# A decoder block on one core: the first adaLN shift group summed by TensorE as columns, its loads in pieces

## Chip, cores and metric

The kernel runs on 1 core of one Trainium2 chip. The metric is the device time of one execution in microseconds (us). The kernel before was timed three times; the median is 1146.56 us.

## What is computed

One decoder block on 256 tokens of width 2048, in float32. A conditioning vector `c` gives six vectors of 2048 values (two shifts, two scales, two gates) through `w_ada`; then come a normalised, scaled and shifted projection `w_in`, eight heads of causal attention beside a gated short convolution, `w_out`, and a gated feed-forward part with a convolution.

```python
mod = jax.nn.silu(c) @ w_ada[l] + b_ada[l]
sh1, sc1, g1, sh2, sc2, g2 = jnp.split(mod, 6, axis=-1)
h = modulate(rms_norm(x, norm1_g[l]), sh1, sc1)      # h * (1 + sc1) + sh1
proj = h @ w_in[l]                                   # 2048 -> 6144
...                                                  # attention | gated convolution, norms
x = x + g1[:, None, :] * (mixed @ w_out[l])
h2 = modulate(rms_norm(x, norm2_g[l]), sh2, sc2)
u = causal_dwconv(h2 @ w_ffn_up[l], ffn_conv_w[l], ffn_conv_b[l])
u_gate, u_up = jnp.split(u, 2, axis=-1)
x = x + g2[:, None, :] * ((jax.nn.silu(u_gate) * u_up) @ w_ffn_down[l])
```

## The kernel before

**Slots.** All weights stream from HBM through seven buffers of 1 MB ("raw"). A weight tile is a *slot*. ScalarE (ACT) rounds it to a high part `hi` (line 329), VectorE (DVE) forms the remainder `lo` (through the wrapper at line 166, under which most DVE work is recorded), and TensorE (PE) makes three products of each block: hi with the high and the low part of the activations, lo with the high part. The first 48 slots are `w_in`, then come 16 of `w_out`, then the feed-forward part. `CFG['turns']` (line 51) lists which columns of the projection (q, k, v, gates g, convolution inputs c and x) the first 48 slots cover, in which order and for which block rows. Slot 0 has its own loop, `go_first` (line 574, matmuls on line 583); later ones use lines 514 to 517.

**The six vectors.** Each of them is cut into groups (class `Ada`, `CFG['ada']`, line 44). A group's tiles are consumed between slots, in one of two ways: by PE (`pe` true: a block of silu(c), repeated over 32 columns, is stationary, the weights move, four row groups at once; line 396) or by DVE, row block by row block (lines 387, 389). `evac` copies a PE group's sums out (line 417), `cols` transposes them by PE (line 453) and sums the four row groups on DVE, so that the values lie along the partitions; B gets shift + bias, A gets (1 + scale) x gain.

**The order.** Everything runs in the order of the program: each engine has one queue. `CFG` sets when a step is placed: `at(i, f)` puts step f at slot i, `cls` puts it before or after that slot's preparation, `x_first` and `hi_late` say for each slot whether adaLN tiles come before the next weights, and whether `hi` is made late. `consume` (a list near the end) is the order of all loads; `load_next` issues the next one on SyncE's queue when a buffer has been given back.

**The head.** Before slot 0 can start, x is loaded and transposed by PE in eight blocks (`xn_tr`), its norm is worked out, and `xn_norm` multiplies each transposed block by it on DVE. In the two groups of `ada_init` (line 1171), the scale SC1 and the shift SH1 of the first 256 columns are summed by PE from two tiles of 1 MB each. SH1 is the last of them (from line 1525): consume its two tiles, `evac`, `cols`; its values z go into `h = hf + z` on ACT (line 1548), where `hf` was made by DVE as x * A1 + bias. Then slot 0's first matmul can go. Slot 0's tile is loaded in two halves (`pair_load`, line 539), and split into hi and lo in two halves, too.

Of the kernel before, what the change touches and what calls it, by code (L numbers as in the profile page):

```python
# [9 lines left out]
F32 = mybir.dt.float32  # L10
F32R = mybir.dt.float32r
AF = mybir.ActivationFunctionType
ALU = mybir.AluOpType
AX = mybir.AxisListType

P = 128
D = 2048
S = 256
NK = D // P
# [9 lines left out]
SH1, SC1, G1, SH2, SC2, G2 = range(6)  # L29
# [11 lines left out]
       'unit_act': [0, 1, 2, 3, 4, 5, 6, 7],  # L41
       'down_turns': [[0, 1, 2], [3]],
       'join': [[-5, 1], [-2, 6]],
       'ada': [[0, 2, 256, False, 0, 5], [2, 0, 2048, False, 26, 22], [5, 0, 2048, False, 40, 32],
# [3 lines left out]
       'bufs': [38, 6, 7, 3, 3],  # L48
       'parked': ['q'],
       'unpark': 56,  # L50
# [5 lines left out]
       'fill': [[3, 12]],  # L56
# [25 lines left out]
               'qk_norm': 0,  # L82
               'out_norm': 0,
               'cols': -1,
               'conv_q': 0,
               'att_q': -1,
               'up_gate': 2,
               'hold_a': 2,
# [7 lines left out]
               'up_conv': 2,  # L96
               'up_conv_b': 2,
               'att_p': 0,
               'ss_part': 0,
               'up_sum': -1,  # L100
               'sq_out': -1,
               'att_s': -1,
               'tr_out': 0,
               'evac': 1,
               'qk_stat': 2,
               'load_x': 1,
               'att_t': 2,
               'att_o': 2,
               'gate_down': 2,
               'conv_g': 1,  # L110
               'conv_c': -1,
               'evac_in': 0,
               'qk_root': 0,
               'evac_out': -1,
               'bias': -1,
               'add_bias': -1,
               'up_silu': 2,
               'ss_cols': -1,
               'sum_rows': 1,
               'evac_sum': -1,  # L120
               'join_load': 0,
               'join_sum': 2},
       'up0': [[1, 1, 2, 4], [0, 1, 3, 3], [0, 2, 1, 2], [1, 1, 3, 5], [4, 4, 5, 8], [5, 5, 6, 9]],
       'la': 2,
       'near': 3,
# [1 line left out]
       'direct': 4,  # L127
       'spill': [6, 9],
       'back': [-2, 0, -1, 1],
       'x_first': [1, 2, 3, 4, 6, 8, 9, 10, 11, 12, 13, 14, 16, 18, 20, 21, 22, 26, 27, 30, 31, 34, 37, 39, 42, 43, 44, 45,  # L130
                   47, 48, 49, 50, 51, 53, 57, 58, 59, 60, 61, 62, 65, 66, 67, 74, 82, 83],
       'h_act': True,
       'h_lag': 0,
       'hi_late': [1, 2, 3, 5, 6, 11, 12, 14, 15, 17, 19, 20, 21, 22, 25, 26, 28, 30, 31, 32, 39, 42, 44, 45, 47, 49, 51,
                   53, 54, 57, 59, 61, 64, 66, 68, 70, 72, 76, 77, 78, 79, 80, 82, 83],
       'first_hi': True,
       'cut': [4, 4, 4],
       'fold': 3,
       'twos': [],
# [8 lines left out]
def tile_block(  # L148
# [5 lines left out]
    nc = tc.nc  # L154
    mm = nc.tensor.matmul
    act = nc.scalar.activation
# [14 lines left out]
    V, W = Vector(), nc.vector  # L171
# [10 lines left out]
    def bank(name):  # L182
        return ps.tile([P, 512], F32, tag="b", bufs=8, name=name)
# [3 lines left out]
    def t2k(name, dt=F32):  # L187
        return sb.tile([P, 512], dt, tag="t2k", bufs=N_T2K, name=name)

    def t1k(name, dt=F32):  # L190
        return sb.tile([P, 256], dt, tag="t1k", bufs=N_T1K, name=name)

    def small(n, name):
        return sb.tile([P, n], F32, tag="small", bufs=16, name=name, padded_shape=[P, 32])
# [64 lines left out]
    def load_next():  # L259
        if not pending:  # L260
            return
        issue, key = pending.pop(0)
        if isinstance(issue, Ada):

            issue.home()
            return
        t = sb.tile([P, 4, 512], F32, tag="raw", bufs=N_RAW, name="raw")
        issue(t)
        ready.append((key, t))

    def take(key):
        n = [k for k, _ in ready].index(key)
        return ready.pop(n)[1]
# [65 lines left out]
    csil = const.tile([P, NK], F32, name="csil")  # L339
    crep = const.tile([P, NK, 32], F32, name="crep")  # L340
    A1 = const.tile([P, NK], F32, name="A1")
# [4 lines left out]
    class Ada:  # L346


        def __init__(self, part, c0, n, pe):
            self.part, self.c0, self.n, self.pe = part, c0, n, pe  # L350
            self.rows = 2048 // n
            self.tiles = NK // self.rows
            self.nch = n // P
            self.acc = None
            self.two = []
            self.used = 0

        def want(self, r):
            a = self.part * D + self.c0 * P
            k0 = r * self.rows  # L360

            def issue(t):
                nc.sync.dma_start(self.view(t), w_ada[0, k0 * P:(k0 + self.rows) * P, a:a + self.n]
                                  .rearrange("(k p) f -> p k f", p=P))
            return issue

        def home(self):
            what = f"ada{self.part}_{self.c0}"
# [112 lines left out]
    def at(i, f, *a):  # L481
        tasks.setdefault(i, []).append((CFG["cls"].get(f.__name__, 0), f, a))

    done = set()
# [3 lines left out]
    hT = {}  # L488
# [5 lines left out]
    COL = {"q0": 0, "q1": 1, "k0": 2, "k1": 3, "v0": 4, "v1": 5, "g0": 6, "g1": 7, "c0": 8, "c1": 9,  # L494
           "x0": 10, "x1": 11}

    def halves(v):
        return v[:, :256], v[:, 256:]
# [21 lines left out]
    for w in CFG["parked"]:  # L520
        q = sb.tile([P, 4, 512], F32, tag="raw", bufs=N_RAW, name="pa_" + w)
# [15 lines left out]
    slots_begun = []  # L537

    def pair_load(k, f):
        def issue(t):  # L540

            n = 1 if not slots_begun else 2
            slots_begun.append(f)
            for j in range(0, 2, n):
                nc.sync.dma_start(t.rearrange("p (k h) f -> p k (h f)", k=2)[:, j:j + n],
                                  w_in[0, (k + j) * P:(k + j + n) * P, COL[f] * 512:COL[f] * 512 + 1024]
                                  .rearrange("(k p) f -> p k f", p=P))
        return issue


    turns, upto = [], {}
# [124 lines left out]
    for n, (f, part, k) in enumerate(seq):  # L676
# [6 lines left out]
        i = len(slots)  # L683
# [411 lines left out]
    for n, (what, *a) in enumerate(CFG["plan"]):  # L1095
        if what == "x":
# [10 lines left out]
            rest = todo  # L1107
# [12 lines left out]
    parts = []  # L1120
    for fs in CFG["down_turns"]:
        k = ka
# [46 lines left out]
        ready_at.update({(g.part, g.c0 + k): s + 2 for k in range(g.nch)})  # L1169

    ada_init = [Ada(SC1, 0, 256, True), Ada(SH1, 0, 256, True)]

    def h_chunks(ks):
        assert all((part, k) in done for k in ks for part in (SC1, SH1))
# [12 lines left out]
    for part, c0 in CFG["fill"]:  # L1187
        g = Ada(part, c0, 512, True)
        fill += [(g, r) for r in range(g.tiles)]
    n0, n1, n2 = CFG["fill_at"]  # L1190
    extra.setdefault(N_OUT - 1, []).extend(fill[:n0])
    fill_a, fill_b = fill[n0:n0 + n1], fill[n0 + n1:n0 + n1 + n2]
    for i, (g, r) in enumerate(fill):
        if i >= n0 + n1 + n2:
            extra.setdefault(N_OUT + (i - n0 - n1 - n2) // 2, []).append((g, r))
        if r == g.tiles - 1:
            a = N_OUT + 1 + max(0, (i - n0 - n1 - n2) // 2)
# [163 lines left out]
    for half in range(2):  # L1361
        for w in "qk":
            at(in_last[f"{w}{half}"], qk_stat, f"{w}{half}")
        i = max(in_last[f"{w}{half}"] for w in "qk")
        at(i + CFG["qk"][half][0], qk_root, half)
        at(i + CFG["qk"][half][1], qk_norm, half)
        n = i + CFG["qk"][half][1]
        for j in range(4):
            h = 4 * half + j
# [82 lines left out]
    for i in range(len(slots)):  # L1452
# [3 lines left out]
        w = [("w", n) for n in ahead(i)]  # L1456
# [29 lines left out]
    xnT, xnP = {}, {}  # L1486
# [13 lines left out]
    g1n, bcol = vbc[:, 0:16], vbc[:, 16:112]  # L1500
# [12 lines left out]
    def xn_norm(*js):  # L1513
        for j in js:
            xnT[j] = t2k(f"xnT{j}")
            V.tensor_tensor(out=xnT[j].rearrange("p (k t) -> p k t", k=2), in0=xnP.pop(j).rearrange("p (k t) -> p k t", k=2),
                            in1=rT.unsqueeze(1).to_broadcast([P, 2, 256]), op=ALU.mult)

    xn_norm(0, 1, 2, 3)
    ada_init[0].consume(1)  # L1520
    ada_init[0].evac()
    ada_init[0].cols()
    xn_norm(4)
    xn_tr(5)
    ada_init[1].consume(0)
    xn_tr(6, 7)
    xn_norm(5, 6, 7)
    ada_init[1].consume(1)
    ada_init[1].evac()

    w = take(("w", 0))
    hi, lo = (sb.tile([P, 4, 512], F32R, tag=g, bufs=N_HL, name=g) for g in ("hi", "lo"))
    parts = [(slice(2 * k, 2 * k + 2), t1k("hf"), t2k(f"h{k}", F32R)) for k in range(2)]
    b1 = SH1 * NK
    for k, (s, h, hk) in enumerate(parts):
        hT[k] = halves(hk)
        V.tensor_scalar(h, xnT[0][:, k * 256:(k + 1) * 256], A1[:, k:k + 1], bcol[:, b1 + k:b1 + k + 1],
                        op0=ALU.mult, op1=ALU.add)  # L1540
    s = parts[0][0]
    if CFG["first_hi"]:
        V.tensor_copy(hi[:, s], w[:, s])
    else:
        act(hi[:, s], w[:, s], AF.Copy)
    z, _ = ada_init[1].cols(True)
    for k, (s, h, hk) in enumerate(parts):
        act(hT[k][0], h, AF.Identity, bias=z[:, k:k + 1])
        if not k:
            act(hi[:, parts[1][0]], w[:, parts[1][0]], AF.Copy)  # L1550
    for k, (s, h, hk) in enumerate(parts):
        V.scalar_tensor_tensor(out=hT[k][1], in0=h, scalar=z[:, k:k + 1], in1=hT[k][0].bitcast(F32),
                               op0=ALU.add, op1=ALU.subtract)
    for s, _, _ in parts:
        V.tensor_tensor(out=lo[:, s], in0=w[:, s], in1=hi[:, s].bitcast(F32), op=ALU.subtract)
    splits.append((hi, lo))
    load_next()
    split_hi(1)
# [100 lines left out]
```

## Time and profile before

| what | us |
|---|---|
| three timed runs | 1147.93, 1146.56, 1146.21 |
| median | 1146.56 |
| the profiled execution | 1145.98 |
| its span, first to last instruction | 1144.2 |
| PE busy | 1129.7 |
| DVE busy | 1064.4 |
| ACT busy | 731.6 |
| start of the first projection matmul (slot 0) | 23.82 |

Times of the trace count from the first instruction of the profiled execution. Rows of the timeline give start, length, engine, line, operation, output and inputs, shape and count; a bracket gives the idle time of the engine just before, and what ended it. Rows of the waits give the total waited, how often, and the longest. "PEclk", or the column after the engines in a table by stretch, is the granted share of TensorE's clock. A float32 product shows as two MATMUL records, a transpose as one.

### The profile page before, as it was taken

The numbers are of one execution on the slowest core, as the hardware profiler recorded it, in microseconds if no ns is written. First come the engines' busy times: TensorE is split into PE (matmuls) and PEld (weight loads), VectorE is DVE, ScalarE is ACT, GpSimd is POOL, SyncE is SP. The second block draws the span as 40 slices with busy tenths as digits, with TensorE's granted clock in tenths as the row PEclk, the third lists the DMA queues.
The fourth block names the chain that finished last, engine by engine and source line by source line (L and its number), as shares of the span: only waits on it lengthen the run. The fifth ranks groups of instructions, "written<-read, shape, count | busy, mean of one in ns | idle before, by whom it ended". The sixth has DMA issues, their size and how long they took to land.

```text
span 1144.2 us, 16252 instructions
## 1 busy us (share of the span) xinstructions
PE 1129.7 (99%) x6035; PEld 954.1 (83%) x6035; DVE 1064.4 (93%) x1167; ACT 731.6 (64%) x1091; POOL 61.5 (5%) x90
## 2 busy tenths in 40 slices
PE   6999999999999999999999999999999999999998
PEld 4777778888888879988888888888888888888887
DVE  4789989989999998889999999899999999999798
ACT  4644455576786555566687676776677768866731
POOL 1000000000000000000000000101011101111000
PEclk8999999999999999999999999999999999999999
DMA  9999998998998899987679887999899988999951
GB/s 361 407 412 397 412 371 302 408 382 308 331 397 314 290 317 359 325 278 245 213 246 369 305 293 248 310 360 299 313 272 340 317 317 265 351 313 303 367 222 74
DMA packets 198687, 363.66 MB, mean 318 GB/s; under 512 B 9408, under 2 KB 108180, under 8 KB 194000
## 3 DMA queue, kind: packets, MB, share of 16 engines
q1 hardware_dynamic: 189152, 343.44, 82.8%
q0 software_dynamic: 8160, 17.04, 6.9%
q10 hardware_dynamic: 1296, 2.16, 0.6%
q8 instruction: 47, 0.77, 0.2%
q14 instruction: 32, 0.26, 0.1%
HBM read 343.70 MB, written 18.89 MB: 317 GB/s over the span
## 4 chain that ended last, share of the span: by engine, by line
PE 94%; DVE 2%; DMA 2%; issue 1%; ACT 1%; SPq 0%; DVEq 0%; ACTq 0%
PE z L1063 24%; PE z L1066 13%; PE u L1002 4%; PE u L1004 4%; PE u L1000 4%; PE z L1048 4%; PE ada L396 1%; DVE lo L166 1%; PE mx L516 1%; PE mq L516 1%; PE mg L516 1%; PE mk L516 1%; PE mx L517 1%; PE mv L516 1%; PE mg L517 1%; PE mq L517 1%
## 5 line engine op out<-in xcount | busy, mean ns | idle before, releaser
L329 ACT ACTIVATE hi<-raw 128x2048 fp32r<-128x2048 f32 (+1 forms) x227 | 417.6, 1857 | 263.6 <-DMA raw<-in_w_in_dram 73.5
L166 DVE TENSOR_TENSOR lo<-raw,hi 128x2048 fp32r<-128x2048 f32 (+2 forms) x229 | 501.6, 2200 | 23.3 <-ACT hi L329 23.1
L1063 PE MATMUL z<-h,hi 128*128 128x512 f32 x1280 | 303.3, 390 | 0.3 <-DVE ub L166 0.3
L1063 PEld LDWEIGHTS z<-h,hi 128*128 128x128 f32 x1280 | 237.8, 188 | 49.5 <-ACT hi L329 0.8
L389 DVE SCALAR_TENSOR_TENSOR ada<-raw,csil,ada 128x512 f32<-128x512 f32 (+3 forms) x167 | 195.7, 1175 | 5.3 <-DMA raw<-in_w_ada_dram 1.8
L1066 PEld LDWEIGHTS z<-h,lo 128*128 128x128 f32 x1280 | 163.1, 191 | 5.6
L1066 PE MATMUL z<-h,lo 128*128 128x256 f32 x1280 | 165.0, 283 | 0.0
L1002 PE MATMUL u<-hi,gh 128*128 128x512 f32 x224 | 88.1, 394 | 0.1
L1004 PE MATMUL u<-hi,gl 128*128 128x512 f32 x224 | 87.7, 392 | 0.0
L1000 PE MATMUL u<-lo,gh 128*128 128x512 f32 x224 | 61.4, 390 | 0.0
L812 ACT ACTIVATE uy<-ub,fc,fc 128x256 f32<-128x256 f32 x88 | 47.6, 599 | 11.9 <-DVE ub L166 11.9
L944 POOL DMA_DIRECT2D down_sums<-pu x42 | 36.7, 1290 | 304.3 <-ACT pu L940 304.3
L1002 PEld LDWEIGHTS u<-hi,gh 128*128 128x128 f32 x224 | 42.2, 188 | 10.0 <-ACT pu L940 2.9
L1000 PEld LDWEIGHTS u<-lo,gh 128*128 128x128 f32 x224 | 41.9, 188 | 9.2 <-DVE lo L166 0.3
L1004 PEld LDWEIGHTS u<-hi,gl 128*128 128x128 f32 x224 | 42.2, 189 | 7.5
L1048 PE MATMUL z<-h,hi 128*128 128x256 f32 x256 | 46.6, 284 | 0.4 <-ACT h L771 0.2
L823 ACT ACTIVATE tap<-ub,fc 128x256 f32<-128x256 f32 x96 | 41.7, 504 | 0.0
L1048 PEld LDWEIGHTS z<-h,hi 128*128 128x128 f32 x256 | 40.0, 192 | 0.8 <-ACT h L771 0.5
L166 DVE TENSOR_TENSOR ub<-z,ub 128x256 f32<-128x256 f32 x96 | 33.8, 414 | 7.2 <-ACT ub L844 7.1
L301 DVE TENSOR_TENSOR raw<-raw 128x1024 f32<-128x1024 f32 x32 | 38.9, 1217 | 1.2 <-DMA raw<-in_w_ffn_down_dram 1.2
L844 ACT ACTIVATE ub<-z 128x256 f32<-128x256 f32 x96 | 28.6, 383 | 12.7 <-PE z L1063 12.7
L1048 PE MATMUL z<-h,lo 128*128 128x256 f32 x128 | 36.2, 283 | 0.0
(460 smaller groups left out, 1787.3 us busy)
## 6 DMA issues: line engine op xcount, KB each, us to landing
raw<-in_w_ada_dram SPq DMA_DIRECT2D x96, 1024.0 KB, 7.4
raw<-in_w_ffn_up_dram SPq DMA_DIRECT2D x176, 512.0 KB, 6.1
raw<-in_w_in_dram SPq DMA_DIRECT2D x47, 1024.0 KB, 8.1
raw<-in_w_ffn_down_dram SPq DMA_DIRECT2D x44, 1024.0 KB, 9.5
raw<-in_w_out_dram SPq DMA_DIRECT2D x16, 1024.0 KB, 5.9
raw<-in_w_ffn_down_dram SPq DMA_DIRECT2D x32, 512.0 KB, 4.9
down_sums<-pu POOLq DMA_DIRECT2D x56, 256.0 KB, 8.0
raw<-in_w_ffn_down_dram SPq DMA_DIRECT2D x32, 256.0 KB, 5.3
```

What stands on the lines that cost most here:

```text
L166: f(*a, **k)
L329: act(hi[:, :n], t[:, :n], AF.Copy)
L389: W.scalar_tensor_tensor(out=self.acc, in0=t[:, j, :], scalar=csil[:, i:i + 1], in1=self.acc, op0=ALU.mult, op1=ALU.add)
L516: mm(o, a, hi[:, k, s], start=(first and k == 0), stop=False)
L812: act(y[:, s], b[:, s], AF.Identity, bias=bias[:, i + j:i + j + 1], scale=w[2][:, i + j:i + j + 1])
L823: act(z[:, s], b[:, s], AF.Copy, scale=w[2 - d][:, i + j:i + j + 1])
L1000: mm(bank_of(key), a, lo[:, n], start=False, stop=j in ends)
L1002: mm(bank_of(key), a, hi[:, n], start=key not in begun, stop=False)
L1004: mm(bank_of(key), b, hi[:, n], start=False, stop=False)
L1048: mm(o, w[:, j, a], h2T[k + j][:, v * 256:v * 256 + 256], start=begins and j == 0 and w is hi and not v, stop=ends and j == 3 and w is lo)
L1063: mm(zp[grp][ft], hi[:, j, ft * P:(ft + 1) * P], h2T[k + j], start=begins and j == 0, stop=ends and j == 3 and not late)
L1066: mm(zp[grp][ft][:, :256], lo[:, j, ft * P:(ft + 1) * P], h2T[k + j][:, :256], start=False, stop=ends and j == 3 and late)
```

## The change

The SH1 group of the head is summed another way. `columns(r, i, j)` takes the weight blocks themselves (128x128, float32) as stationary operands and moves one column of silu(c), `csil[:, n:n+1]`; the sum of each block of 128 columns arrives as one PSUM column, so that neither `evac` nor `cols` is needed. One DVE addition of the bias gives z. The group's second tile is loaded in two pieces (rows 0 to 5 and 6 to 7 of its eight), the first weight tile in four (it was two) and rounded in four pieces, three by DVE and one by ACT. `hf` is x * A1 without the bias and is made as soon as A1 is there. The normalising products are placed at three points (`norm_at` = 2, 7, 7): two before the scale group ends, blocks 2 to 4 after hf, 5 and 6 before the shift sum, block 7 after the pieces of lo.

The rest of the table: in `turns` v and g of the second and third slot change places, and `v, 2, 4` moves behind `g1` and `k1`; the second tiles of two adaLN groups come a little earlier (spans 5 to 4 and 2 to 1: for the latter, both tiles now follow slot 1); `unpark` goes from 56 to 58; `x_first` and `hi_late` have other members from slot 7 on; some classes of `cls` change. No matmul of a weight slot is added or removed.

```diff
-       'ada': [[0, 2, 256, False, 0, 5], ...
+       'ada': [[0, 2, 256, False, 0, 4], ...
-               [1, 2, 256, True, 1, 2], ...
+               [1, 2, 256, True, 1, 1], ...
-       'turns': [['c', 0, 2], ['v', 0, 2], ['g', 0, 2], ['x', 0, 2], ...
+       'turns': [['c', 0, 2], ['g', 0, 2], ['v', 0, 2], ['x', 0, 2], ...
+       'norm_at': [2, 7, 7],
...
             def issue(t):
-                nc.sync.dma_start(self.view(t), w_ada[0, k0 * P:(k0 + self.rows) * P, a:a + self.n]
-                                  .rearrange("(k p) f -> p k f", p=P))
+                for i, j in self.cuts.get(r, [(0, self.rows)]):
+                    nc.sync.dma_start(self.view(t)[:, i:j], w_ada[0, (k0 + i) * P:(k0 + j) * P, a:a + self.n]
+                                      .rearrange("(k p) f -> p k f", p=P))
+
+        def columns(self, r, i, j):
+            if i == 0:
+                self.used += 1
+                self.held = self.view(take((self, r)))
+            if self.acc is None:
+                self.acc = bank(f"adap{self.part}_{self.c0}")[:, :self.nch]
+            for k in range(i, j):
+                for b in range(self.nch):
+                    n = self.rows * r + k
+                    mm(self.acc[:, b:b + 1], self.held[:, k, b * P:(b + 1) * P], csil[:, n:n + 1],
+                       start=n == 0 and b == 0, stop=n == NK - 1 and b == self.nch - 1)
+            if j == self.rows:
+                load_next()
...
+            if not slots_begun:
+                slots_begun.append(f)
+                for j in range(4):
+                    a = (COL[f] + j % 2) * 512
+                    nc.sync.dma_start(t[:, j], w_in[0, (k + j // 2) * P:(k + j // 2 + 1) * P, a:a + 512])
+                return
...
+    ada_init[1].cuts[1] = [(0, 6), (6, 8)]
...
-    xn_norm(0, 1, 2, 3)
-    ada_init[0].consume(1)
-    ada_init[0].evac()
-    ada_init[0].cols()
-    xn_norm(4)
+    xn_norm(*range(n0))
+    sc.consume(1)
+    sc.evac()
+    sc.cols()
+    for k in range(2):
+        hf.append(t1k("hf"))
+        V.tensor_scalar(hf[k], xnT[0][:, k * 256:(k + 1) * 256], A1[:, k:k + 1], None, op0=ALU.mult)
+    xn_norm(*range(n0, 5))
     xn_tr(5)
-    ada_init[1].consume(0)
+    sh.columns(0, 0, 8)
     xn_tr(6, 7)
-    xn_norm(5, 6, 7)
-    ada_init[1].consume(1)
-    ada_init[1].evac()
+    xn_norm(*range(5, n1))
+    sh.columns(1, 0, 6)
+    sh.columns(1, 6, 8)
...
-    z, _ = ada_init[1].cols(True)
+    V.tensor_tensor(out=z, in0=sh.acc, in1=bcol[:, b1:b1 + 2], op=ALU.add)
...
+    V.tensor_copy(hi[:, 0], w[:, 0])
+    rest(0)
+    V.tensor_copy(hi[:, 1], w[:, 1])
+    rest(1)
+    act(hi[:, 2], w[:, 2], AF.Copy)
+    V.tensor_copy(hi[:, 3], w[:, 3])
+    xn_norm(*range(n1, n2))
+    for j in range(0, 4, 2):
+        V.tensor_tensor(out=lo[:, j:j + 2], in0=w[:, j:j + 2], in1=hi[:, j:j + 2].bitcast(F32), op=ALU.subtract)
+    xn_norm(*range(n2, 8))
```

More of the change, by code (lines that the diff above doesn't have):

```diff
@@ L43 @@
        'join': [[-5, 1], [-2, 6]],
-       'ada': [[0, 2, 256, False, 0, 5], [2, 0, 2048, False, 26, 22], [5, 0, 2048, False, 40, 32],
+       'ada': [[0, 2, 256, False, 0, 4], [2, 0, 2048, False, 26, 22], [5, 0, 2048, False, 40, 32],
                [0, 8, 512, True, 11, 12], [3, 8, 512, False, 55, 7], [4, 0, 1024, False, 23, 22], [0, 4, 512, True, 4, 6],
                [0, 12, 512, False, 17, 4], [1, 4, 512, False, 3, 7], [4, 12, 512, False, 67, 8], [1, 8, 1024, False, 9, 8],
[1 row of a table removed]
[1 row of a table added]
        'bufs': [38, 6, 7, 3, 3],
        'parked': ['q'],
-       'unpark': 56,
[3 rows of a table removed]
+       'unpark': 58,
[3 rows of a table added]
                  ['q1', 8, 12], ['q1', 12, 16], ['k1', 8, 16], ['v1', 8, 16], ['c0', 8, 16], ['x0', 8, 16], ['g0', 8, 16],
@@ L84 @@
                'cols': -1,
-               'conv_q': 0,
+               'conv_q': 2,
                'att_q': -1,
@@ L98 @@
                'att_p': 0,
-               'ss_part': 0,
+               'ss_part': -1,
                'up_sum': -1,
@@ L105 @@
                'qk_stat': 2,
-               'load_x': 1,
+               'load_x': -1,
                'att_t': 2,
@@ L110 @@
                'conv_g': 1,
-               'conv_c': -1,
+               'conv_c': 0,
                'evac_in': 0,
@@ L115 @@
                'bias': -1,
-               'add_bias': -1,
+               'add_bias': 0,
                'up_silu': 2,
@@ L121 @@
                'join_load': 0,
-               'join_sum': 2},
+               'join_sum': 1},
        'up0': [[1, 1, 2, 4], [0, 1, 3, 3], [0, 2, 1, 2], [1, 1, 3, 5], [4, 4, 5, 8], [5, 5, 6, 9]],
@@ L129 @@
        'back': [-2, 0, -1, 1],
-       'x_first': [1, 2, 3, 4, 6, 8, 9, 10, 11, 12, 13, 14, 16, 18, 20, 21, 22, 26, 27, 30, 31, 34, 37, 39, 42, 43, 44, 45,
-                   47, 48, 49, 50, 51, 53, 57, 58, 59, 60, 61, 62, 65, 66, 67, 74, 82, 83],
+       'x_first': [1, 2, 3, 4, 6, 8, 10, 11, 12, 18, 19, 21, 22, 26, 30, 31, 34, 37, 39, 42, 43, 44, 47, 48, 49, 50, 53, 55,
+                   57, 58, 59, 60, 61, 65, 66, 67, 68, 69, 73, 74, 76, 81, 82, 83],
        'h_act': True,
        'h_lag': 0,
-       'hi_late': [1, 2, 3, 5, 6, 11, 12, 14, 15, 17, 19, 20, 21, 22, 25, 26, 28, 30, 31, 32, 39, 42, 44, 45, 47, 49, 51,
-                   53, 54, 57, 59, 61, 64, 66, 68, 70, 72, 76, 77, 78, 79, 80, 82, 83],
+       'hi_late': [1, 2, 3, 5, 7, 11, 12, 14, 15, 16, 19, 20, 21, 22, 25, 26, 30, 31, 32, 34, 35, 39, 42, 45, 51, 53, 54,
+                   57, 58, 59, 64, 66, 72, 76, 77, 78, 80, 82, 83],
        'first_hi': True,
+       'norm_at': [2, 7, 7],
        'cut': [4, 4, 4],
@@ L356, in __init__ @@
             self.used = 0
+            self.cuts = {}
         def want(self, r):
@@ L540, in issue @@
         def issue(t):
[L542 to L547, printed above, removed]
+            if not slots_begun:
[4 more added lines that the diff above has]
+                return
+            nc.sync.dma_start(t.rearrange("p (k h) f -> p k (h f)", k=2),
+                              w_in[0, k * P:(k + 2) * P, COL[f] * 512:COL[f] * 512 + 1024]
+                              .rearrange("(k p) f -> p k f", p=P))
         return issue
@@ L1517, in xn_norm @@
                             in1=rT.unsqueeze(1).to_broadcast([P, 2, 256]), op=ALU.mult)
-    xn_norm(0, 1, 2, 3)
-    ada_init[0].consume(1)
-    ada_init[0].evac()
-    ada_init[0].cols()
-    xn_norm(4)
+    sc, sh = ada_init
+    n0, n1, n2 = CFG["norm_at"]
+    xn_norm(*range(n0))
+    sc.consume(1)
+    sc.evac()
+    sc.cols()
+    hf = []
+    b1 = SH1 * NK
+    for k in range(2):
+        hf.append(t1k("hf"))
+        V.tensor_scalar(hf[k], xnT[0][:, k * 256:(k + 1) * 256], A1[:, k:k + 1], None, op0=ALU.mult)
@@ L1524, in tile_block @@
+    xn_norm(*range(n0, 5))
     xn_tr(5)
-    ada_init[1].consume(0)
+    sh.columns(0, 0, 8)
     xn_tr(6, 7)
-    xn_norm(5, 6, 7)
-    ada_init[1].consume(1)
-    ada_init[1].evac()
+    xn_norm(*range(5, n1))
+    sh.columns(1, 0, 6)
+    sh.columns(1, 6, 8)
     w = take(("w", 0))
     hi, lo = (sb.tile([P, 4, 512], F32R, tag=g, bufs=N_HL, name=g) for g in ("hi", "lo"))
[L1535 to L1545, printed above, removed]
-    z, _ = ada_init[1].cols(True)
[L1547 to L1552, printed above, removed]
-                               op0=ALU.add, op1=ALU.subtract)
@@ L1554, in tile_block, with rest @@
-    for s, _, _ in parts:
-        V.tensor_tensor(out=lo[:, s], in0=w[:, s], in1=hi[:, s].bitcast(F32), op=ALU.subtract)
+    z = small(8, "adaz")[:, :2]
+    V.tensor_tensor(out=z, in0=sh.acc, in1=bcol[:, b1:b1 + 2], op=ALU.add)
+    done.update((SH1, k) for k in range(2))
+    hk = [t2k(f"h{k}", F32R) for k in range(2)]
+    for k in range(2):
+        hT[k] = halves(hk[k])
+        act(hT[k][0], hf[k], AF.Identity, bias=z[:, k:k + 1])
+    V.tensor_copy(hi[:, 0], w[:, 0])
+    def rest(k):
+        V.scalar_tensor_tensor(out=hT[k][1], in0=hf[k], scalar=z[:, k:k + 1], in1=hT[k][0].bitcast(F32),
+                               op0=ALU.add, op1=ALU.subtract)
```

8 rows, old and new, of the table CFG are left out of this document.

## The prediction

> **What bounds the kernel now.** I read the page first, then who TensorE waits for, then the first 31 us instruction by instruction, then the granted clock window by window. The page:
>
> ```profile
> span 1144.2 us, 16252 instructions
> PE 1129.7 (99%) x6035; PEld 954.1 (83%) x6035; DVE 1064.4 (93%) x1167; ACT 731.6 (64%) x1091; POOL 61.5 (5%) x90
> PE 94%; DVE 2%; DMA 2%; issue 1%; ACT 1%; SPq 0%; DVEq 0%; ACTq 0%
> ```
>
> TensorE is busy for 99% and carries 94% of the chain that ended last. A busy PE need not be a streaming PE, so I ask for its waits from 24 us to the end:
>
> ```profile
> PE mc L583 <- ACT h L1548: 1.1, 1, 1.1
> PE z L1063 <- DVE ub L166: 0.3, 1, 0.3
> PE z L1048 <- ACT h L771: 0.2, 1, 0.2
> ```
>
> The 1.1 us is the wait that ends with the first projection product at 23.82 us. After it, PE waits 0.5 us in all. So the kernel is a head of about 24 us and then a line of matmuls that never stops. Whatever delays the start of that line arrives at the end in full, since no later pause can absorb it. The head, from the timeline:
>
> ```profile
> 15.98 2.48 DVE L166 TENSOR_TENSOR xnT<-xn,n1rT 128x512 f32<-128x512 f32 x4 [1.55 <-ACT n1rT L1511]
> 17.89 0.44 PE L453 MATMUL adac<-ident,adae 128*128 128x128 f32 x2 [0.51 <-ACT adae L417]
> 18.17 0.60 PE L1495 MATMUL xn<-ident,xr 128*128 128x128 f32 x4
> 18.38 0.16 DVE L166 TENSOR_REDUCE adaz<-adac 128x2 f32<-128x8 f32 x1
> 18.70 1.07 PE L396 MATMUL ada<-raw,crep 128*32 128x256 f32 x16
> 18.77 0.16 DVE L166 TENSOR_TENSOR A<-adaz,vbc 128x2 f32<-128x2 f32 x1
> 19.70 1.09 PE L1495 MATMUL xn<-ident,xr 128*128 128x128 f32 x8
> 20.73 1.07 PE L396 MATMUL ada<-raw,crep 128*32 128x256 f32 x16
> 21.82 0.73 DVE L166 TENSOR_SCALAR hf<-xnT,A,vbc 128x256 f32<-128x256 f32 x2
> 21.86 0.38 ACT L417 ACTIVATE adae<-ada 128x256 f32<-128x256 f32 x1 [4.02 <-PE ada L396]
> 22.30 0.44 PE L453 MATMUL adac<-ident,adae 128*128 128x128 f32 x2 [0.50 <-ACT adae L417]
> 23.06 0.16 DVE L166 TENSOR_REDUCE adaz<-adac 128x2 f32<-128x8 f32 x1
> 23.26 0.51 ACT L1548 ACTIVATE h<-hf,adaz 128x256 fp32r<-128x256 f32 x1 [1.01 <-DVE adaz L166]
> 23.82 5.59 PE L583 MATMUL mc<-hi,h 128*128 128x512 f32 x16 [1.08 <-ACT h L1548]
> 29.25 1.98 PE L583 MATMUL mc<-lo,h 128*128 128x512 f32 x8
> 31.07 0.39 PE L516 MATMUL mv<-hi,h 128*128 128x512 f32 x1
> ```
>
> The two shift tiles (18.70, 20.73) take PE 1.0 us each. Then come evacuation, transposes, the sum on DVE, and h: from the start of the DVE sum to the first product 23.82 - 23.06 = 0.76 us. Slot 0, 24 products, takes 31.07 - 23.82 = 7.25 us, while its last eight run at about (31.07 - 29.25) / 8 = 0.227 us each, which would make 5.45. The clock explains the difference:
>
> ```profile
> 7.60:11.01 3.41, 3.39 (x17) 1.00 1.04 374
> 11.01:14.43 3.42, 1.60 (x21) 1.00 1.09 385
> 14.43:17.84 3.41, 2.96 (x20) 0.50 1.09 379
> 17.84:21.25 3.41, 3.35 (x42) 1.00 1.06 416
> 21.25:24.67 3.42, 1.83 (x17) 1.00 1.02 414
> 24.67:28.08 3.41, 3.41 (x9) 0.50 1.03 399
> 28.08:31.49 3.41, 3.41 (x16) 1.00 1.09 386
> ```
>
> Columns: stretch, length, PE busy (count), granted clock, DMA share, GB/s. The clock changes on a 3.41 us grid, and a stretch's clock follows the busy time of the one before: after 2.96, 3.35, 3.39 and 3.41 us it is full, after 1.60 and 1.83 it is half. The gap before slot 0 costs it half a clock from 24.67 to 28.08. (The clock record begins near 11 us, so the 1.00 of the first row says nothing: its 17 products took 3.41 / 17 = 0.20 us each, the half-clock pace.)
>
> **The change, part by part.**
>
> *The shift group as columns.* Each of the two tiles goes from 8 products of 256 moving columns to 16 products of one moving column, each with a 128x128 float32 block as stationary operand. The trace has this very form once, the sums of squares:
>
> ```profile
> 349.30 0.94 PE L1333 MATMUL ssA<-ones,sq 128*128 128x1 f32 x8
> 350.11 0.49 PE L516 MATMUL m('C', 0)0_3055<-hi,mixh 128*128 128x512 f32 x1
> L1333 PE MATMUL ssA<-ones,sq x8: 164/250/250, 349.3 to 350.0; 128*128 128x1 f32 x8
> ```
>
> Four float32 products stand there as 8 records, from 349.30 to 350.11: 0.81 us, that is 0.10 (over 8) to 0.116 (over 7, since the first weight load lay under the matmul ahead). I take 0.11. A one-column product costs its weight load. So a tile is 32 records x 0.11 = 3.5 us where 1.0 was, and the two 7.0 us. The Trainium skill (TensorE: Matmul & The Clock Gate, Back-to-back issue gap) would speak for the change instead: it gives some 60 cycles, 25 ns, for 1 to 64 free columns, by which both tiles together would be an estimated 1.6 us. By that the first product would be no later than now; the row decides for 0.11.
>
> Now the chain. PE is free for the first tile at 18.70, as now (the bank it needs is that of an early transposed block, normalised by then). 18.70 + 3.5 = 22.2; the eight transposes of x took 20.73 - 19.70 = 1.03, to 23.25; 24 records of the second tile 2.64, to 25.9; its last 8 another 0.88, to 26.8. The last record's own 0.25 ends near 26.9. One DVE addition now gives the shift (evacuation, two transposes and the reduction are gone) and starts at about 26.97; plus the 0.76 above, the first product is at 27.73: **3.9 us later** than 23.82. The removed steps had cost 23.06 - 20.73 - 1.0 = 1.3 us; the added weight loads cost 5.
>
> *Clock of slot 0.* If one-column products count as busy, 21.25 to 24.67 is full and 24.67 to 28.08 has about 2.4 + 0.3 = 2.7 busy us. That lies between 1.83 (half follows) and 2.96 (full follows), nearer the latter: I take full. Slot 0 then takes 5.45 instead of 7.25: **-1.8**. At half clock in the next window it would give back 1.6.
>
> *Load in pieces.* The second shift tile and the first weight tile:
>
> ```profile
> L363 SPq DMA_DIRECT2D raw<-in_w_ada_dram x1: 2632/2632/2632, 9.6 to 9.6; - x1
> DMA to landing us min/median/max: 10.8/10.8/10.8
> L545 SPq DMA_DIRECT2D raw<-in_w_in_dram x2: 432/1570/2707, 12.2 to 15.0; - x2
> DMA to landing us min/median/max: 7.9/8.6/9.4
> ```
>
> The shift tile lands at 9.6 + 10.8 = 20.4, the two halves of the weight tile by 15.0 + 7.9 = 22.9. PE reaches the second shift tile at 23.25. Everything has landed by then, so splitting buys nothing, whichever piece comes first: 0. The three added issues cost at least 0.43 us of SP each, behind a queue that is full (DMA share above 1.0 in the rows above): 0, at worst 1.3 us on a transfer that has slack now that PE is late. If PE were not late, the same pieces could be worth up to 20.73 - 20.4 = 0.3 us.
>
> *DVE's order.* Two normalising products of 0.62 (2.48 / 4) come first, then the scale columns until 18.93, two hf of 0.37 until 19.7, five more products until about 22.9, all before the shift sum. That is under PE's 26.97, so moving products back costs 0 and hides 0; if PE's part were short, DVE would set 22.9 as the earliest start of the sum. After it, DVE makes in turn the pieces of hi, the two h remainders (0.49 each), lo and the eighth product; the third matmul waits for the first remainder, which is ready 0.5 us after h and is wanted after two matmuls, 0.45: **+0.1**. The lo of slot 1 ends near 35.0 and is wanted at 33.3 + 1.8 = 35.1: 0, with little to spare; 0 to +0.7 as bounds.
>
> *The rest of the table* (turns, order classes, which loads come first). PE's matmuls stay the same in number. What it could win is the 0.5 us of waits above and some 0.2 from two shift tiles in one group; what it could lose is a wait of about the same size as those seen: -0.5 to +1, taken as **-0.1**.
>
> Sum: +3.9 - 1.8 + 0.1 - 0.1 = **+2.1 us**. The profiled execution took 1145.98 us (span 1144.2), so it would take 1148.1. The three timed runs have 1146.56 as median, 0.58 above it; against them I expect **1148.6**.
>
> **The rivals.**
>
> *Slot 0 stays at half clock.* The 2.7 busy us may not suffice: +1.6 more, +3.7, so 1150.3. For it: 1.83 did not suffice. Against: 2.96 did.
>
> *One-column products do not count as activity.* Then 17.84 to 21.25 holds only about 1 us of transposes and half clock sets in at 21.25. By then (21.25 - 18.70) / 0.11 = 23 records are done; 9 at 0.21 reach 23.2, the transposes 24.9, the second tile's 32 records 31.6, the first product 32.6. It starts at half clock until 34.9 or 38.3 on the grid: slot 0 ends at 39.2 to 40.8 against 31.07. That is +8.1 to +9.7, 1154.7 to 1156.3. Nothing in the trace shows a stretch of such products long enough to decide. The Trainium skill (the same page, Part 4: PE-mode transpose) says that a form of product, the transpose, does not count as busy in the same way; here the row 7.60:11.01, transposes nearly alone, was followed by full clock, which speaks against such exceptions.
>
> *Not slower: the weight loads are hidden.* To reach slot 1 by 31.07 with a full clock, the first product must start by 25.5, the sum by 24.75, so 64 records have (24.75 - 0.3 - 1.03 - 18.70) = 4.7 us: the point is 0.074 us a record. Well below it, DVE's 22.9 rules and the first product comes at 23.66. The gain is then capped by a transfer:
>
> ```profile
> L363 SPq DMA_DIRECT2D raw<-in_w_ada_dram x1: 367/367/367, 48.6 to 48.6; - x1
> DMA to landing us min/median/max: 13.5/13.5/13.5
> 62.61 0.64 PE L396 MATMUL ada<-raw,crep 128*32 128x512 f32 x4
> ```
>
> A tile that lands at 48.6 + 13.5 = 62.1 is used at 62.61, in both kernels with the same tiles loaded ahead of it by a full queue. PE can win no more than 0.5 us before it waits there: 1146.0 to 1146.4. Against: the 0.81 us above.
>
> **How the numbers follow.** A measurement tells about 0.2% (2.3 us) from no change; the bound lies at 1148.85. Chances: forecast 0.43, slot 0 at half clock 0.13, no activity counted 0.24, hidden loads 0.13, surprises of the rest of the table 0.07. The forecast's own range is 1147.7 to 1149.6 (the bounds of its small terms) and two fifths of it lie past the bound. Slower by over 0.2%: 0.17 + 0.13 + 0.24 + 0.02 = 0.56. Within: 0.26 + 0.10 + 0.02 = 0.38. Faster: 0.06, from hidden loads and surprises, as the cap leaves little. The range takes in all three rivals but their ends: 1146.1 to 1156.0.
>
> **What would show it.** Right: 64 one-column records at 0.10 to 0.12 us between 18.7 and 27 us, first product near 27.7, full clock from 28.1, PE's waits after that below 1 us, slot 1 at about 33.2. Wrong: records at 0.21 (no activity), half clock during slot 0, records under 0.074, or new waits of PE after 33 us, which would mean that the rest of the table matters more than the head.

## The result, and the profile after

The changed kernel takes **1154.55 us** in the median of six runs (1152.44 to 1156.97); six runs of the kernel before, in turn with them, have a median of 1146.16 us. The ratio is 1.0073, with a 95% interval of 1.0059 to 1.0088: 8.4 us slower. The profiled execution took 1154.83 us, with a span of 1153.0, against 1145.98 and 1144.2 before. One execution of all those below, of the kernel with the new head alone, took 2910 us and is left out of its median and ratio. The predicted range, 1146.1 to 1156.0, holds the time and the sign is right; but the range was drawn to take in all the rivals, and the likeliest case, +2.1 us, is not what happened. What happened is the second rival: one-column products did not count as activity for the clock, +8.1 to +9.7.

First the page of the changed kernel: span, busy times, and who carries the chain that ended last.

```profile
span 1153.0 us, 16320 instructions
PE 1139.3 (99%) x6065; PEld 966.5 (84%) x6065; DVE 1064.6 (92%) x1169; ACT 730.0 (63%) x1090; POOL 61.5 (5%) x90
PE 88%; DVE 8%; issue 1%; ACT 1%; DMA 1%; DVEq 0%; SPq 0%; ACTq 0%
```

TensorE (PE) has thirty matmul records more and is busy 9.6 us longer, 1139.3 against 1129.7. That is more than the whole loss, so the loss is not a wait of PE. DVE's and ACT's busy times are as before to within 2 us. PE's waits from the shift sum to the end agree:

```profile
PE mc L603 <- ACT h L1567: 0.8, 1, 0.8
PE z L1083 <- DVE ub L167: 0.3, 1, 0.3
...
```

The wait before the first projection product is 0.8 us now (1.1 before); the longest after it, 0.3 us, was there before, and the two rows left out are 0.2 us each. The time must lie in slow work, and the timeline of the head shows where:

```profile
17.42 5.42 PE L379 MATMUL adap<-csil,raw 128*128 128x1 f32 x32 [0.30 <-DVE A L167]
22.70 1.95 PE L1516 MATMUL xn<-ident,xr 128*128 128x128 f32 x8
...
24.44 6.83 PE L379 MATMUL adap<-csil,raw 128*128 128x1 f32 x32
31.31 0.16 DVE L167 TENSOR_TENSOR adaz<-adap,vbc 128x2 f32<-128x2 f32 x1 [6.35 <-PE adap L379]
...
32.06 5.85 PE L603 MATMUL mc<-hi,h 128*128 128x512 f32 x16 [0.79 <-ACT h L1567]
37.75 1.99 PE L603 MATMUL mc<-lo,h 128*128 128x512 f32 x8
39.57 0.39 PE L533 MATMUL mg<-hi,h 128*128 128x512 f32 x1
```

The second tile's 32 one-column records take 6.83 us, 0.213 us each, where the forecast had 0.11. The first projection product starts at 32.06 us and slot 1 at 39.57 us: 8.50 us later than the 31.07 of before, of the 8.8 us by which the span has grown. DVE waits 6.35 us for the shift sum, so that PE alone sets its time. The granted clock, on its own grid of 3.41 us (columns: stretch, length, PE busy and count, granted clock, DMA share, GB/s):

```profile
15.70:19.12 3.42, 2.61 (x26) 1.00 1.10 385
19.12:22.53 3.41, 3.41 (x18) 0.50 1.06 412
22.53:25.94 3.41, 3.41 (x18) 0.50 1.02 417
25.94:29.36 3.42, 3.42 (x17) 0.50 1.06 388
29.36:32.77 3.41, 2.62 (x11) 0.50 1.08 385
32.77:36.18 3.41, 3.41 (x10) 0.50 1.08 408
36.18:39.60 3.42, 3.42 (x17) 1.00 0.99 348
```

From 19.12 to 36.18 the clock stands at half for five stretches. In three of them the records keep PE busy for 3.41 of 3.41 us and the clock after them is half all the same. It is full again only after 32.77 to 36.18, a whole stretch of the 512-column matmuls of slot 0. Read so, this is the rule of the prediction (a stretch's clock follows the busy time of the one before) with an exception: busy with one-column products is not busy. Whether it is the products, and not something else in the change, is for the experiments.

### The profile page after: what moved, and what is told of

Read it like the earlier page. It is cut to its first block, busy times and chain, and to the rows that moved or that the text cites. A ratio compares the mean times of both kernels' runs of the same rounds, so it can differ in the third digit from the quotient of the medians.

```text
span 1153.0 us, 16320 instructions
## 1 busy us (share of the span) xinstructions
PE 1139.3 (99%) x6065; PEld 966.5 (84%) x6065; DVE 1064.6 (92%) x1169; ACT 730.0 (63%) x1090; POOL 61.5 (5%) x90
## 4 chain that ended last, share of the span: by engine, by line
PE 88%; DVE 8%; issue 1%; ACT 1%; DMA 1%; DVEq 0%; SPq 0%; ACTq 0%
PE z L1083 24%; PE z L1086 13%; PE u L1022 4%; PE u L1020 4%; PE u L1024 4%; PE z L1068 4%; DVE lo L167 4%; DVE ada L406 2%; PE mq L533 1%; PE mv L533 1%; PE mx L533 1%; PE mg L533 1%; PE mk L533 1%; PE mq L534 1%; PE mx L534 1%
```

## The experiments

**Theory:** the clock's gate (whatever sets the granted clock) does not see one-column products as activity; at half clock the group and slot 0 both run slowly, and PE passes the delay on in full. **Rivals:** the rest of the change (order of the head, pieces, table) makes the loss; or the longer group of weight loads makes it by itself, whatever the clock. Each kernel was timed beside the kernel before, whose medians were 1146.05 to 1146.39 us; a ratio with its 95% interval in brackets compares the two.

**All of the change but the columns.** Pieces, order of the head and table are kept; the shift group is summed as before.

```diff
-    sh.columns(0, 0, 8)
+    sh.consume(0)
...
-    sh.columns(1, 0, 6)
-    sh.columns(1, 6, 8)
+    sh.consume(1)
+    sh.evac()
...
-    V.tensor_tensor(out=z, in0=sh.acc, in1=bcol[:, b1:b1 + 2], op=ALU.add)
+    z, bias = sh.cols(True)
+    V.tensor_tensor(out=z, in0=z, in1=bias, op=ALU.add)
```

> The changed kernel with one thing undone: the shift group is summed as before (repeated silu(c) stationary, weights moving, then evacuation, transposes and the sum on DVE); pieces, order of DVE and the rest of the table stay. If the columns are the whole cost: first product at 23 to 24 us, at most 1.5 us after it lost to half clock, no new wait of PE, time within 0.1% of before (1145.5 to 1147.5). If the new table, the pieces or the moved products cost part of the 8.4 us: 1148 or more, with waits of PE after 30 us.

Measured: 1148.04 us (11 runs), ratio 1.0017 [1.0008, 1.0026]. Some 1.7 us of loss are left, 6.5 are gone with the columns. Slot 1 starts at 27.72 us, 3.3 us earlier than in the profile of before, but PE then has waits that the changed kernel does not have, of which the longest is for a load:

```profile
PE ada L413 <- DMA raw<-in_w_ada_dram: 1.3, 1, 1.3
```

**The columns alone**, in the kernel before, with its loads, order and table.

```diff
-    ada_init[1].consume(0)
+    ada_init[1].columns(0, 0, 8)
...
-    ada_init[1].consume(1)
-    ada_init[1].evac()
+    ada_init[1].columns(1, 0, 8)
...
-    z, _ = ada_init[1].cols(True)
+    z = small(8, "adaz")[:, :2]
+    V.tensor_copy(z, ada_init[1].acc)
```

> The kernel before with the columns alone; its loads, its order and its table stay. If the columns are the whole cost: 64 records, nearly all at 0.21 us, half clock from about 19 to 36 us, first product at 31 to 33 us, time 1153.5 to 1156.5. If the rest carries part of it: clearly under 1153.

Measured: 1154.45 us (4 runs), ratio 1.0071 [1.0054, 1.0087], the whole loss. Its timeline:

```profile
17.60 4.25 PE L376 MATMUL adap<-csil,raw 128*128 128x1 f32 x32
...
23.45 6.83 PE L376 MATMUL adap<-csil,raw 128*128 128x1 f32 x32
...
38.03 0.39 PE L530 MATMUL mv<-hi,h 128*128 128x512 f32 x1
```

The same 6.83 us for the second tile, and slot 1 at 38.03. So the loss comes with the columns, and neither the pieces nor the table are needed for it. Slot 1 starts 1.5 us earlier than in the profile of the changed kernel, and yet the spans are 1152.9 and 1153.0 us, so it loses more later; in the feed-forward part, for one, PE waits 0.4 us for ACT and 0.4 us for DVE here, and not there. The two losses, 8.1 us for the columns alone and 1.7 for all the rest, are together more than the 8.4 of the whole change, so they are not shares of it: the waits of the rest come with its early start, and the late start of the whole change does not have them.

**More moving columns, same weight loads.** If the gate does not see a product with one moving column, then the same product with more columns must be seen. `csil`'s column is moved 128 times; all 128 results are equal, and one of them is used. This adds work and takes none away.

```diff
-                    mm(self.acc[:, b:b + 1], self.held[:, k, b * P:(b + 1) * P], csil[:, n:n + 1],
+                    mm(self.acc[:, b * WIDE:(b + 1) * WIDE], self.held[:, k, b * P:(b + 1) * P],
+                       csil[:, n:n + 1].to_broadcast([P, WIDE]),
...
-    V.tensor_tensor(out=z, in0=sh.acc, in1=bcol[:, b1:b1 + 2], op=ALU.add)
+    V.tensor_tensor(out=z, in0=sh.acc[:, ::WIDE], in1=bcol[:, b1:b1 + 2], op=ALU.add)
```

> The changed kernel, but each of its products moves the column of silu(c) 128 times over (the same weight blocks and weight loads, the same sums, 128 equal columns of each, one of which is used). Theory (a one-column product leaves the array idle for the clock's monitor, whatever the weight loads do): full clock through the group, 64 records at 0.11 us, first product near 27 us, time 1147.5 to 1150.5, so 4 to 7 us faster than the changed kernel although it does more. Rival (the half clock came from the light stretch before the group, and its weight loads keep it): records at 0.21 again, 1153 to 1157.

Measured: 1148.18 us (10 runs), ratio 1.0013 [1.0004, 1.0022]. More work in the same place is 6.4 us faster than the change as it was. Its timeline, then its clock:

```profile
16.95 3.81 PE L380 MATMUL adap<-csil,raw 128*128 128x128 f32 x32 [0.40 <-DMA raw<-in_w_ada_dram]
...
21.47 3.74 PE L380 MATMUL adap<-csil,raw 128*128 128x128 f32 x32
26.00 3.98 PE L605 MATMUL mc<-hi,h 128*128 128x512 f32 x16 [0.79 <-ACT h L1569]
31.63 0.39 PE L535 MATMUL mg<-hi,h 128*128 128x512 f32 x1
```

```profile
...
19.41:22.83 3.42, 3.42 (x34) 1.00 1.05 410
22.83:26.24 3.41, 2.62 (x23) 1.00 1.03 422
26.24:29.65 3.41, 3.41 (x16) 1.00 1.07 382
```

Full clock, 3.74 us for a tile's 32 records (0.11 each, as forecast), 2.62 us busy that are followed by full clock, slot 0 in 31.63 - 26.00 = 5.63 us. Neither the order nor the weight loads differ from the changed kernel; both rivals fall as causes of the greater part. Where is the limit? A quarter and a half of the width:

```diff
-WIDE = 128
+WIDE = 32
```

> As wide_128 with 32 columns: the moving part is then about a quarter of each record. If the monitor counts moving columns with a threshold between 0.54 and 0.87 of a stretch: half clock as with one column, 1153 to 1157. If any steady stream of products suffices that is longer than one column: full clock, 1147.5 to 1150.5.

Measured: 1153.28 us (4 runs), ratio 1.0056 [1.0040, 1.0071]. The timeline of the kernel with 32 columns, and its clock:

```profile
23.44 6.87 PE L380 MATMUL adap<-csil,raw 128*128 128x32 f32 x32
...
38.98 0.39 PE L535 MATMUL mg<-hi,h 128*128 128x512 f32 x1
```

```profile
15.50:18.91 3.41, 2.97 (x25) 1.00 1.09 384
18.91:22.32 3.41, 3.41 (x18) 0.50 1.07 414
```

```diff
-WIDE = 128
+WIDE = 64
```

> The changed kernel with the column of silu(c) moved 64 times over: about half of each record is then moving columns. 128 kept the full clock, 32 did not. If the monitor's threshold lies between 0.54 and 0.87 of a stretch and counts moving columns: half clock, 1152 to 1156. If it lies under a half: full clock, 1147 to 1149.5.

Measured: 1148.84 us (10 runs), ratio 1.0019 [1.0010, 1.0028]. With 64 columns:

```profile
15.57:18.98 3.41, 2.98 (x25) 1.00 1.10 387
18.98:22.39 3.41, 3.41 (x33) 1.00 1.06 409
22.39:25.81 3.42, 2.65 (x24) 1.00 1.02 420
25.81:29.22 3.41, 3.39 (x8) 0.50 1.06 385
```

32 columns do not hold the clock, 64 do while the group runs. The first stretches of the two are alike, 2.97 and 2.98 us busy from about 15.5 on, and the next is half with 32 and full with 64. At the end of the group 64 is too little: its stretch with 2.65 us busy is followed by half clock, while 128 columns with 2.62 us are followed by full. So what counts lies nearer to how much is moved than to how long PE is occupied. The limit expected for 64 columns, between 0.54 and 0.87 of a stretch with about half of each record taken as moving, is not borne out, as the clock stayed full in the group. The places of the grid differ a little between these runs, so no finer limit is drawn from them.

**The wide columns without the rest of the change**: 128 equal columns in the kernel with the columns alone, against which the edit is:

```diff
-                    mm(self.acc[:, b:b + 1], self.held[:, k, b * P:(b + 1) * P], csil[:, n:n + 1],
+                    mm(self.acc[:, b * WIDE:(b + 1) * WIDE], self.held[:, k, b * P:(b + 1) * P],
+                       csil[:, n:n + 1].to_broadcast([P, WIDE]),
...
-    V.tensor_copy(z, ada_init[1].acc)
+    V.tensor_copy(z, ada_init[1].acc[:, ::WIDE])
```

> The kernel before with the shift group as columns alone, each product moving its column 128 times; loads, order of the products and table as before. With 128 equal columns in the changed kernel, slot 1 began at 31.63 us (before: 31.07) and yet the time was 1148.18, 1.9 over the kernel before. Theory A, the rest of the change (order of the head, table) makes those 1.9: columns that keep the clock full cost nothing, so slot 1 begins at 31 to 32 us and the time is 1146.0 to 1147.2. Theory B, the longer group of products itself costs them (its tiles are given back later, which shifts the loads): 1147.8 to 1149. By both the 64 records go at 0.11 us each.

Measured: 1147.20 us (11 runs), ratio 1.0008 [0.9999, 1.0017].

```profile
17.71 3.74 PE L377 MATMUL adap<-csil,raw 128*128 128x128 f32 x32
22.16 3.74 PE L377 MATMUL adap<-csil,raw 128*128 128x128 f32 x32
...
32.31 0.39 PE L532 MATMUL mv<-hi,h 128*128 128x512 f32 x1
```

It falls on the edge of what the first theory allowed, and its interval just takes in no change. Against the columns alone, the pair that differs in nothing but the width, it is 1154.45 - 1147.20 = 7.25 us faster. Of the 1.9 us that the changed kernel with 128 columns still loses, about 1 us is gone without the rest of the change; with intervals of this size the split is not firm.

**The rest of the change, in two halves.** The new table in the kernel before, and the new head (its pieces and order, sums as before) with the old table. The table's edit is the whole table of the change without `norm_at`, of which two lines:

```diff
-       'unpark': 56,
+       'unpark': 58,
...
-               'join_sum': 2},
+               'join_sum': 1},
```

The head's edit takes the kernel of the first experiment and puts the old table back, but for one line:

```diff
        'first_hi': True,
+       'norm_at': [2, 7, 7],
```

> The kernel before with only the new table (turns, classes, load order, adaLN spans); head, loads and shift sum as before. Theory that the new table costs what rest_only lost (1148.04 against 1146.30): 1147.3 to 1149, with waits of PE after 40 us that before does not have. Rival (it is the new order of the head, whose earlier start is given back): 1145.5 to 1147.

> The kernel before with the new order of the head and its pieces, the shift group summed as before, and the old table. Theory that the new table costs what rest_only lost: 1145.3 to 1146.5; an earlier slot 1 (28 to 30 us) that is mostly given back where PE waits for an adaLN tile by 62 us, since the loads do not come sooner. Rival (the head's order costs it): 1147.3 to 1149.

Measured: the table alone 1147.03 us (11 runs), ratio 1.0004 [0.9995, 1.0013]; the head alone 1147.2 us (10 runs), ratio 1.0007 [0.9998, 1.0016]. Both times lie between the two cases of their expectations, and neither can be told from no change; together they made 1.7 us. Yet the head alone starts slot 1 at 27.93 us, 3.1 us earlier than the profile of before. Where do these go? Three rows of PE in the kernel with the head alone, and then the row of before for the tile of the first of them:

```profile
41.75 1.07 PE L413 MATMUL ada<-raw,crep 128*32 128x256 f32 x16 [0.37 <-DMA raw<-in_w_ada_dram]
...
46.73 0.50 PE L533 MATMUL mx<-hi,h 128*128 128x512 f32 x1 [0.52 <-ACT pa_g L548]
...
62.12 1.07 PE L413 MATMUL ada<-raw,crep 128*32 128x512 f32 x8
```

```profile
43.30 1.07 PE L396 MATMUL ada<-raw,crep 128*32 128x256 f32 x16
```

And, of the kernel with the head alone, the issue of the tile used at 62.12, with its time to landing:

```profile
48.55 0.37 SPq L366 DMA_DIRECT2D raw<-in_w_ada_dram  x1
...
raw<-in_w_ada_dram SPq DMA_DIRECT2D x1, 1024.0 KB, 13.4
```

PE now waits 0.37 us for a tile at 41.75 and 0.52 us for a copy of ACT at 46.73, and 0.2 us each for DVE and ACT before. Of the 3.1 us at slot 1, 43.30 - 41.75 = 1.55 are left at the first of these rows and 62.61 - 62.12 = 0.5 at the last. That is the size of the cap of the prediction's third rival, but not by its cause: the tile used at 62.12 landed at 48.55 + 13.4 = 61.95, and the row has no wait. By then other waits had taken the gain back. Behind the longest of them is a load all the same. ACT rounds a weight tile just ahead of the copies that PE waits for, and it waits for that tile's load until 44.28 us, in before until 44.33:

```profile
44.28 1.92 ACT L330 ACTIVATE hi<-raw 128x2048 fp32r<-128x2048 f32 x1 [4.05 <-DMA raw<-in_w_in_dram]
```

```profile
44.33 1.92 ACT L329 ACTIVATE hi<-raw 128x2048 fp32r<-128x2048 f32 x1 [4.04 <-DMA raw<-in_w_in_dram]
```

PE starts 3.1 us sooner and the loads do not, so PE waits for what stands behind them.

**Testing the cap.** If the queue of loads takes the gain back at that tile, the time should fall when the group is placed one slot later.

```diff
-               [0, 12, 512, False, 17, 4], [1, 4, 512, False, 3, 7], [4, 12, 512, False, 67, 8], [1, 8, 1024, False, 9, 8],
+               [0, 12, 512, False, 17, 4], [1, 4, 512, False, 4, 6], [4, 12, 512, False, 67, 8], [1, 8, 1024, False, 9, 8],
```

> As head_only, with one adaLN group that DVE sums (scale, blocks 4 to 7) begun one slot later, so that the tile which PE waits for by 62 us lands one transfer (about 2.6 us) sooner. If the queue of loads is what takes the head's gain back: that wait goes, and the time is 0.5 to 1.5 us under head_only (the next tile, by 43 us, has only 1.5 us to spare in the trace of before). If the gain is lost elsewhere: as head_only.

Measured: 1147.76 us (11 runs), ratio 1.0013 [1.0004, 1.0022]. It is not the 0.5 to 1.5 us under the head alone that the cap demands; the other case of the expectation holds, that the gain is lost elsewhere. The wait for a load at 41.75 has stayed (0.4 us). The matmuls around 62 us do come earlier (an adaLN tile is used at 61.37 there), but by 74 us they are no earlier than before; PE's waits there have a new one, for DVE:

```profile
PE mk L533 <- DVE pa_c L167: 0.4, 1, 0.4
```

No version beats the kernel before: an earlier start is not what it lacks. That loads take the early start back is shown for the head alone up to some 47 us; what makes DVE late at 72 us here was not tried.

**The two kernels once more, for how far one execution differs from the next.**

> The kernel before once more, unchanged, for a second profile. Theory that the head's clock and the waits after 700 us vary from execution to execution by as much as the experiments differ from the first profile there: another clock pattern in the head (slot 1 anywhere from 28 to 31 us), the same place by 62 us within 0.6 us, and the last stretch (from 426 us to the end, 717.9 us in the first profile) longer by up to 1.5 us. Rival: that stretch is 717.9 within 0.2 us again, and the other kernels' 718.4 to 720 are theirs.

> The changed kernel once more, unchanged. Theory (one-column products never release the clock): half clock again from within the group until a full stretch of slot 0's products has passed, first product at 30 to 33 us, whatever the phase of the clock's grid; the last stretch 717.5 to 719.5 us.

> The kernel before unchanged, one more look. Its two profiles so far took 717.8 us from the first up matmul to the end, the other kernels 717.9 to 719.9, the changed kernel 718.4 and 719.3 in two looks. If the last stretch is a property of the program, 717.6 to 718.0 again; if it is the execution's, something up to 719.

Measured: the kernel before 1146.10 and 1145.79 us, the changed one 1153.63. In both new profiles of the kernel before, the clock is full from 15 us on, where the first had two stretches at half. The second of them:

```profile
22.24 2.18 PE L583 MATMUL mc<-hi,h 128*128 128x512 f32 x8 [0.80 <-ACT h L1548]
...
28.41 0.39 PE L516 MATMUL mv<-hi,h 128*128 128x512 f32 x1
```

Slot 1 starts at 28.41 us, 2.7 us before that of the first profile, and the executions end within 0.4 us of each other (spans 1144.2, 1144.3, 1144.0): an earlier start is taken back here, too. In the changed kernel's second profile, the first tile of columns ran wholly at full clock, since the grid lay otherwise (its timeline, then its clock):

```profile
16.92 3.70 PE L379 MATMUL adap<-csil,raw 128*128 128x1 f32 x32 [0.30 <-DVE A L167]
21.63 6.83 PE L379 MATMUL adap<-csil,raw 128*128 128x1 f32 x32
...
37.38 0.39 PE L533 MATMUL mg<-hi,h 128*128 128x512 f32 x1
```

```profile
17.67:21.09 3.42, 3.42 (x33) 1.00 1.09 405
21.09:24.50 3.41, 3.41 (x20) 0.51 1.03 416
```

This is the plainest case: a stretch at full clock that the records fill wholly, most of it with one-column products, is followed by half clock. The first projection product starts at 29.25 us, a little before the 30 to 33 that were expected. Slot 1 is 2.2 us earlier than in the first profile, the span 1.2 us shorter. The place of the grid would explain a part of the spread of the changed kernel's runs. The last stretch, from the first up matmul (426.32 us in the first profile of before) to the end, took 717.8, 717.8 and 718.4 us in the three profiles of the kernel before, 718.4 and 719.3 in the two of the changed one. It is thus no property of the program alone.

## Why the prediction was right, and where it was not

**The step that failed** is the one on the clock: "If one-column products count as busy, 21.25 to 24.67 is full ... I take full." They do not count. The prediction had the alternative as a rival at 0.24, with nothing in the trace long enough to decide, and its working there was good: first product 32.6 (measured 32.06), end of slot 0 at 39.2 to 40.8 (39.57), time +8.1 to +9.7 (8.85 between the two profiled executions, 8.4 between the medians). That the first product came so near has some luck in it: half clock set in at 19.12, not 21.25 us, which made the first tile 0.8 us longer than this rival had it, and the group began 1.28 us sooner.

**Term by term**, forecast against the profile:

- The group starts at 17.42, not 18.70 us: -1.28. The 18.70 belonged to one execution, with half clock from 14.43 to 17.84; the two later profiles of the kernel before have 17.01 and 16.79.
- First tile, until the transposes: 22.70 - 17.42 = 5.28 us against 3.5 (half clock from 19.12 on): +1.78.
- The eight transposes: 24.44 - 22.70 = 1.74 against 1.05 (22.2 to 23.25): +0.69.
- Second tile, until the sum: 31.31 - 24.44 = 6.87 against 3.72 (23.25 to 26.97): +3.15.
- From the sum to the first product: 0.75 against 0.76. These five make the first product 4.3 us later than the forecast's 27.73.
- Slot 0: 39.57 - 32.06 = 7.51 against 5.45: +2.1. The term "-1.8" became +0.3.

That is 6.4 us at slot 1, and 1154.83 - 1148.1 = 6.7 us at the end.

**What held.** 64 records, each the price of its weight load, at 0.11 us under full clock (the first tile of the changed kernel's second profile: 3.7 us for 32). The kernels with 128 columns are the forecast's own case, and gave 1148.18 and 1147.20 us against its 1148.6. The stretch at the start of slot 0, where it counted 2.7 busy us and took full clock, has 2.62 with 128 columns and is followed by full; with 64 columns 2.65 were not enough. In the changed kernel DVE hides all that was moved onto it: it waits 6.35 us before the sum. The last piece of the tile and the pieces of the weight tile are not waited for. A start delayed by 8.5 us arrives as 8.8.

**What was too simple.** "Whatever delays the start of that line arrives at the end in full" holds for a delay beyond the 31 us of the first profile, not for a gain: there, PE comes to wait for loads and for copies behind loads. The third rival's cap, 0.5 us at 62 us, had the right size, but PE does not wait at that tile, and loading it sooner did not bring the time down. The price of before's own half clock, 1.8 us in slot 0, was taken as something to win back; in two other executions of that kernel it is not there and the end is the same. The 128-column sum of +2.1 came near the measured one with this term in it, so the agreement says less than it seems to.

**The price of a record, and what the clock watches.** The row gave 0.11 us for a one-column product, and the changed kernel shows 0.11 and 0.213. The Trainium skill (TensorE: Matmul & The Clock Gate, Back-to-back issue gap) gives 25 ns for 1 to 64 columns. The prediction left out that the page means the gap of an isolated matmul there, and that the same section has both set the pace in a stream of weight loads and matmuls. This group is such a stream, each record with the load of a 128x128 block, and none shows the 25 ns. The Trainium skill (the same page, Part 1: The HAM clock gate) says that the gate watches how busy PE is, over stretches of some 3.4 us; the grid agrees, but after three stretches here that the records fill wholly the clock stays at half, so the busy time that the records show is not the quantity watched. The Trainium skill (the same page, Part 4: PE-mode transpose) says that transposes do not count as busy in the same way; in the profile of before a stretch of transposes nearly alone was followed by full clock, and the form that does not count is the product with one or with 32 columns under such a load.

**What stays open.** With 128 columns the changed kernel still loses 1.9 us (0.5 to 2.5 by its interval), and the start accounts for little of it: slot 1 begins 0.56 us later than in the first profile of before. In its profile, and in that of the head alone, the feed-forward part has short waits of PE for DVE that the first profile of before lacks. The head alone, about 150 us before its end:

```profile
990.15 0.39 PE L1022 MATMUL u<-hi,gh 128*128 128x512 f32 x1
990.92 0.49 PE L1024 MATMUL u<-hi,gl 128*128 128x512 f32 x1 [0.38 <-DVE gl L167]
```

What makes DVE late there was not tried; such waits differ from one execution of the same program to the next, too. What exactly the gate counts (columns moved, or the array's share of time in use) was not tried either.

## What to carry to other kernels

Here a product that moves one column costs its weight load, and a run of them lets the clock fall to half for itself and for what comes after, although the profile shows PE busy: where such a group takes longer than one stretch of the clock's grid, read the granted clock stretch by stretch, not the busy share. If the form is wanted, move equal columns beside the one that is needed: they are free under the weight load (0.11 us with 1 or with 128) and keep the clock. And before an earlier start is priced, look whether the loads behind it come sooner, too: here they did not, and 3.1 us gained at slot 1 were 0.5 us by 62 us and nothing at the end.

## What was not expected of the hardware

More columns cost no time: a record with 1 and one with 128 moving columns both take 0.11 us at full clock. The one-column record slows with the clock, from 0.11 to 0.213 us, and so does its weight load (from 0.19 to 0.33 us in the profile of the changed kernel). And with the same weight loads, the moving width decides the clock of a row of such products: half with 1 and 32 columns, full with 64 and 128.
